# Rotary embedding of queries and keys: the sine half added in DRAM by transfers that exchange the halves

## The chip, the cores and the metric

The kernel runs on one core of a Trainium2 chip. The metric is the device time of one execution in microseconds. Three runs of the kernel before took 2127.07, 2130.25 and 2131.83 us; the median is 2130.25 us.

The engines are named as in the profile: PE multiplies matrices (PEld is its loading of weights), DVE is the vector engine, ACT the scalar engine, POOL is GpSimd, SP is SyncE. Here SP issues nearly all transfers, and POOL issues those that add to what is at their destination.

## The reference

One layer of an encoder on two sequences that share the weights: a long one of 1024 tokens (`x_sample`) and a short one of 512 (`x_prompt`), model width 2048, all in float32. The input is normalised and multiplied by one wide `w_in`, whose columns are split into a convolution group (value, GLU gate, output gate), Q (8 heads of 128), K and V (2 heads each), and an attention gate. The convolution group goes through a depthwise convolution of 31 taps, a layer norm and a 1024 x 1024 product. Q and K are rotated by position; attention looks at bands of 128 tokens on either side, with a sink. Both groups are gated, joined, multiplied by `w_out`, added to the input and normalised. The part that is touched:

```python
def apply_rope(t, pos):
    half = HEAD_DIM // 2
    inv_freq = 1.0 / (ROPE_THETA ** (jnp.arange(half, dtype=jnp.float32) / half))
    ang = pos.astype(jnp.float32)[:, None] * inv_freq[None, :]
    cos = jnp.cos(ang)[None, :, None, :]
    sin = jnp.sin(ang)[None, :, None, :]
    tf = t.astype(jnp.float32)
    t1, t2 = tf[..., :half], tf[..., half:]
    out = jnp.concatenate([t1 * cos - t2 * sin, t2 * cos + t1 * sin], axis=-1)
    return out.astype(t.dtype)
```

## The kernel before

**Layout.** Activations are kept transposed: the 128 channels of a head lie on the 128 partitions, tokens along the row, 512 at a time (`W`). The two halves of a head are therefore rows 0 to 63 and 64 to 127. The table `cos` holds the cosines twice; `sin` holds the sines in its upper half and their negatives in its lower half.

**Products.** Every float32 operand is split into a high part (ACT, line 438) and a low part (DVE, line 439), and three products of the parts are summed on PE. The long sequence is multiplied in blocks of 2 x 2 x 2 with seven products instead of eight (class `Unit`, line 191). One unit takes a pair of column blocks, such as Q of a head and its attention gate, over half of the 2048 input channels. Its seven products leave four sums, one for each half of the tokens (t) and each of the two column blocks (c). In the first pass the sums go to DRAM (`part_...`). In the second pass `finish` (line 240) adds the stored part to the new one with an adding transfer on POOL (`add_into`, line 429) and enters `done` in a list (`later`), which is worked off four products later: for Q and K that is `rotate` (line 943), for gates `silu_of`, for V `value_of`.

**Order.** The second passes of the long sequence stand in the order gates 0 to 3, K and V of two groups, the eight Q units, gates 4 to 7. Then come the products of the short sequence (class `Job`, line 578), the first of them its K, V and Q, each with 48 matrix products, rotated by `rotated` (line 940) straight out of PE's bank. Beside these products run lanes of background work that a clock of estimated costs hands out: the taps of the convolution on DVE (line 906), attention of the long sequence, and preparation. `turn_over` and `behind` tie such work to places in the instruction streams; a scheduler then orders each engine's instructions.

**Buffers.** Tiles named g and u are [128, 512] (four each), taken in turn by `E()`. Tiles of the tag a (four, line 399) hold up to [128, 1024]. Near the end of the second pass, `last_before` (line 1713) loads the normalised input of the short sequence from DRAM (`xr_d`) for splitting: the first eight channel blocks into four a tiles (line 1703), the next four into p tiles (line 1700).

**Rotation before.** `rope` (line 928) multiplies each half of the rows by the sines of the other into b, multiplies all rows by the cosines into o, and adds b to o: four DVE instructions. The result is stored by SP. Q and K are read again later, when attention reaches them.

Of the kernel before, what the change touches and what calls it, by code (L numbers as in the profile page):

```python
# [7 lines left out]
F32 = mybir.dt.float32  # L8
F32R = mybir.dt.float32r
AF = mybir.ActivationFunctionType  # L10
ALU = mybir.AluOpType
PSUM = bass.MemoryType.PSUM

P = 128
# [19 lines left out]
W = 512  # L34
# [619 lines left out]
class Sequence:  # L654
# [270 lines left out]
            nc.vector.tensor_tensor(self.cos, self.cos, self.R, ALU.mult)  # L925
            nc.vector.tensor_tensor(self.sin, self.sin, self.R, ALU.mult)

    def rope(self, acc, c, o=None):
        e, nc = self.e, self.e.nc
        i = slice(c * W, c * W + W)  # L930
        if o is None:
            o = e.G()
        b = e.E()
        nc.vector.tensor_tensor(b[0:64], acc[64:128], self.sin[64:128, i], ALU.mult)
        nc.vector.tensor_tensor(b[64:128], acc[0:64], self.sin[0:64, i], ALU.mult)
        nc.vector.tensor_tensor(o, acc, self.cos[:, i], ALU.mult)
        nc.vector.tensor_tensor(o, o, b, ALU.add)
        return o

    def rotated(self, dst, accs):  # L940
        self.e.store(dst, self.rope(accs[0], 0))

    def rotate(self, dst):
        def done(t, z):
            self.e.store(dst[:, t * W : t * W + W], self.rope(z, t, z))
            yield

        return done
# [902 lines left out]
```

## Time and profile before

The profiled execution took 2123.9 us, of which the span from the first to the last instruction is 2122.1 us, at a granted TensorE clock of 0.998. It is 6.35 us below the median of the three runs.

| engine | busy us | share of the span | instructions |
|---|---|---|---|
| PE | 2080.0 | 98% | 9330 |
| PEld | 1709.6 | 81% | 9330 |
| DVE | 1710.3 | 81% | 2611 |
| ACT | 1064.6 | 50% | 1736 |
| POOL | 105.1 | 5% | 124 |

| stretch (us) | PE busy | DVE busy | DMA share | what runs |
|---|---|---|---|---|
| 640 to 840 | 198.66 | 193.81 | 0.71 | second pass of K, V and Q, long sequence |
| 840 to 870 | 26.83 | 23.79 | 0.94 | last gates; splitting of the short sequence's input |
| 870 to 1050 | 175.54 | 169.64 | 0.52 | K, V and Q of the short sequence, attention of the long one |

How to read it: a share over the whole span mixes stages with different limits. DMA share is the mean busy share of the 16 DMA engines; it can read a little over 1. A wait is idle time of an engine just before an instruction, with what ended it.

### The profile page before, as it was taken

What the parts mean: (1) busy time and instruction counts of PE and PEld (TensorE: products, weight loads), DVE (VectorE), ACT (ScalarE), POOL (GpSimd) and SP (SyncE); (2) the same over time, 40 slices, a digit from 0 to 9 for tenths busy, and PEclk for the clock granted to TensorE, in tenths of its full rate; (3) what the DMA queues carried; (4) which work ended last, traced back from release to release, by engine and by line L of the source; (5) the groups of instructions that cost most, each with busy time, mean ns of one, the idle gap of its engine ahead of it and who ended that gap; (6) DMA issues with size and microseconds to landing.
All of it is one profiled execution on the core that took longest, in us unless ns stands there. A gap on an engine that the chain in (4) does not pass through costs nothing. (4 is left out here: it accounts for less than half of the span.)

```text
span 2122.1 us, 26838 instructions
## 1 busy us (share of the span) xinstructions
PE 2080.0 (98%) x9330; PEld 1709.6 (81%) x9330; DVE 1710.3 (81%) x2611; ACT 1064.6 (50%) x1736; POOL 105.1 (5%) x124
## 2 busy tenths in 40 slices
PE   8999999999999999899999999999999989999998
PEld 7878888888888888688888888878888867888886
DVE  8758799988899999899987776677899667987543
ACT  7475445333554444544556766345544564563232
POOL 0001110000011111000000000000000001110000
PEclk9999999999999999999999999999999999999999
DMA  8888878754677767754464547987765369799952
GB/s 286 310 286 243 231 179 277 265 190 155 227 215 178 185 161 194 240 183 144 151 219 157 192 157 235 323 291 255 249 238 199 105 208 269 192 306 314 309 172 80
DMA packets 236408, 465.17 MB, mean 219 GB/s; under 512 B 22128, under 2 KB 79856, under 8 KB 236272
## 3 DMA queue, kind: packets, MB, share of 16 engines
q1 hardware_dynamic: 218992, 431.99, 60.6%
q0 software_dynamic: 17280, 31.46, 9.0%
q8 instruction: 73, 1.20, 0.2%
q14 instruction: 63, 0.52, 0.1%
HBM read 319.19 MB, written 144.18 MB: 218 GB/s over the span
## 5 line engine op out<-in xcount | busy, mean ns | idle before, releaser
L191 PE MATMUL a<-t,hl 128*128 128x512 f32 x2640 | 634.3, 391 | 15.5 <-ACT u L217 6.0
L191 PEld LDWEIGHTS a<-t,hl 128*128 128x128 f32 x2640 | 494.7, 188 | 123.4 <-ACT u L217 9.2
L438 ACT ACTIVATE hl<-raw 128x1024 fp32r<-128x1024 f32 (+1 forms) x330 | 296.2, 898 | 367.8 <-DVE raw L138 66.7
L439 DVE TENSOR_TENSOR hl<-raw,hl 128x1024 fp32r<-128x1024 f32 (+1 forms) x330 | 337.6, 1023 | 171.0 <-ACT hl L438 167.0
L906 DVE SCALAR_TENSOR_TENSOR f<-f,c_w_dw,f 128x1024 f32<-128x1024 f32 (+1 forms) x464 | 456.0, 1011 | 1.8 <-ACT f L901 1.6
L578 PE MATMUL a<-t,hl 128*128 128x512 f32 x1344 | 329.0, 394 | 2.6 <-DVE f L848 2.2
L191 PE MATMUL c<-t,hl 128*128 128x512 f32 x1320 | 320.1, 390 | 1.6 <-ACT g L217 0.9
L578 PEld LDWEIGHTS a<-t,hl 128*128 128x128 f32 x1344 | 248.8, 188 | 53.8 <-DVE f L848 2.6
L191 PEld LDWEIGHTS c<-t,hl 128*128 128x128 f32 x1320 | 247.4, 188 | 54.0 <-ACT g L217 1.8
L578 PE MATMUL c<-t,hl 128*128 128x512 f32 x672 | 167.4, 395 | 0.0
L578 PE MATMUL b<-t,hl 128*128 128x512 f32 x672 | 162.2, 392 | 0.8 <-DVE hl L439 0.8
L191 PE MATMUL b<-t,hl 128*128 128x512 f32 x660 | 161.1, 390 | 0.0
L578 PEld LDWEIGHTS b<-t,hl 128*128 128x128 f32 x672 | 125.1, 188 | 26.1 <-DVE hl L439 1.2
L578 PEld LDWEIGHTS c<-t,hl 128*128 128x128 f32 x672 | 124.2, 188 | 24.5
L191 PEld LDWEIGHTS b<-t,hl 128*128 128x128 f32 x660 | 123.4, 188 | 25.1
L217 ACT ACTIVATE u<-a 128x512 f32<-128x512 f32 x114 | 67.3, 592 | 77.7 <-PE a L191 64.5
L217 ACT ACTIVATE g<-a 128x512 f32<-128x512 f32 x106 | 62.9, 593 | 80.8 <-PE a L191 68.9
L1534 PE MATMUL a<-hl,t 128*128 128x512 f32 x192 | 74.3, 390 | 0.0
L438 ACT ACTIVATE a<-pt 128x512 fp32r<-128x512 f32 x64 | 38.0, 594 | 62.5 <-PE pt L1058 62.3
L1038 ACT ACTIVATE p<-p,tiny 128x384 f32<-128x384 f32 (+1 forms) x96 | 54.5, 569 | 28.3 <-DVE tiny L1035 19.5
L346 ACT ACTIVATE hl<-raw 128x1024 fp32r<-128x1024 f32 x44 | 46.4, 1053 | 41.1 <-PE a L578 12.7
L439 DVE TENSOR_TENSOR a<-pt,a 128x512 fp32r<-128x512 f32 x64 | 43.9, 686 | 25.3 <-ACT a L438 24.9
(318 smaller groups left out, 2528.2 us busy)
## 6 DMA issues: line engine op xcount, KB each, us to landing
raw<-w_in SPq DMA_DIRECT2D x171, 512.0 KB, 5.0
raw<-w_out SPq DMA_DIRECT2D x64, 256.0 KB, 4.2
raw<-w_out SPq DMA_DIRECT2D x31, 512.0 KB, 4.7
raw<-w_pw SPq DMA_DIRECT2D x24, 512.0 KB, 4.8
p<-xT_s SPq DMA_DIRECT2D x40, 256.0 KB, 4.8
f<-x_s SPq DMA_DIRECT2D x16, 512.0 KB, 7.2
f<-y_d SPq DMA_DIRECT2D x16, 512.0 KB, 5.8
y_s<-f SPq DMA_DIRECT2D x16, 512.0 KB, 4.5
```

What stands on the lines that cost most here:

```text
L191: nc.tensor.matmul(acc, hl[:, l, o, j, :], toks[j][:, r], start=name in FRESH and j == 0 and q == 0, stop=name in LAST and j == HALF - 1 a ...
L217: nc.scalar.activation(t, bank, AF.Copy)
L346: e.nc.scalar.activation(t[:, 0], raw, AF.Copy)
L438: nc.scalar.activation(hi, x, AF.Copy)
L439: nc.vector.tensor_tensor(lo, x, hi.bitcast(F32), ALU.subtract)
L578: nc.tensor.matmul(job.acc[0], hl[:, l, kk // HALF, kk % HALF, :], r, start=i == 0 and p == 0, stop=i == nk - 1 and p == 2,)
L906: nc.vector.scalar_tensor_tensor(t, h[:, j : j + T], w(j), t, ALU.mult, ALU.add)
L1038: nc.scalar.activation(p[:, 0:n], p[:, 0:n], AF.Exp, bias=nm[:, h : h + 1], accum_out=l[:, h : h + 1])
L1534: nc.tensor.matmul(acc, self.mix[self.KS[i]][:, m, b * P : (b + 1) * P], part[l].rearrange("p a b -> p (a b)"), start=i == 0 and p == 0, s ...
```

## The change

The sum of the cosine and sine products moves from DVE into DRAM. `rope` now multiplies all 128 rows by the cosines and all 128 rows by the sines, each row by its own, and adds nothing. `put_rotated` stores the cosine product as before (SP) and then adds to it, with two adding transfers on POOL, the lower half of the sine product to the upper rows and the upper half to the lower rows. For the long sequence the sine product lies in a tile of tag a in place of one from `E()`; for the short sequence it is still one from `E()`.

```diff
-    def rope(self, acc, c, o=None):
-        e, nc = self.e, self.e.nc
+    def rope(self, acc, c, o, b):
+
+        nc = self.e.nc
         i = slice(c * W, c * W + W)
-        if o is None:
-            o = e.G()
-        b = e.E()
-        nc.vector.tensor_tensor(b[0:64], acc[64:128], self.sin[64:128, i], ALU.mult)
-        nc.vector.tensor_tensor(b[64:128], acc[0:64], self.sin[0:64, i], ALU.mult)
+        nc.vector.tensor_tensor(b, acc, self.sin[:, i], ALU.mult)
         nc.vector.tensor_tensor(o, acc, self.cos[:, i], ALU.mult)
-        nc.vector.tensor_tensor(o, o, b, ALU.add)
-        return o
 
     def rotated(self, dst, accs):
-        self.e.store(dst, self.rope(accs[0], 0))
+        e = self.e
+        o, b = e.G(), e.E()
+        self.rope(accs[0], 0, o, b)
+        self.put_rotated(dst, o, b)
+
+    def put_rotated(self, dst, o, b):
+        e, half = self.e, P // 2
+        e.store(dst, o)
+        e.add_into(dst[0:half], b[half:])
+        e.add_into(dst[half:], b[0:half])
 
     def rotate(self, dst):
         def done(t, z):
-            self.e.store(dst[:, t * W : t * W + W], self.rope(z, t, z))
+            b = self.e.A([W], F32)
+            self.rope(z, t, z, b)
+            self.put_rotated(dst[:, t * W : t * W + W], z, b)
             yield
 
         return done
```

POOL's queue in the last Q unit and the first gate unit after it, before the change. The destination is on the left of the arrow; `part_q7_10` is the stored sum of Q head 7, second half of the tokens (1), column block Q (0). Waits on DMAHW are for SP's transfers, on DMASW for POOL's own.

```order
L429 DMA u_887_6976<-part_q7_11_407 128x512 [waits DMAHW1_49,DMASW5_49,DVE_49]
L429 DMA g_883_6936<-part_q7_01_405 128x512 [waits DMASW6_49,DVE_49]
L429 DMA u_893_7025<-part_q7_10_406 128x512 [waits DMAHW1_49,DMASW7_49,Activation_49]
L429 DMA g_897_7047<-part_gate4_00_338 128x512 [waits DMAHW2_49,DMASW0_49,DVE_49]
L429 DMA g_904_7124<-part_gate4_11_341 128x512 [waits DMAHW7_49,DMASW1_49,DVE_49]
L429 DMA u_900_7084<-part_gate4_01_339 128x512 [waits DMAHW4_49,DMASW2_49,DVE_49]
```

The same place in the changed kernel; `a_888` and `a_901` are the sine products of the two halves of the tokens, `q_d0_1` is Q of the second group in DRAM.

```order
L429 DMA u_887_6976<-part_q7_11_407 128x512 [waits DMASW1_49,DVE_49]
L429 DMA u_883_6936<-part_q7_01_405 128x512 [waits DMAHW7_49,DMASW2_49,DVE_49]
L429 DMA g_893_7025<-part_q7_10_406 128x512 [waits DMAHW3_49,DMASW3_49,Activation_49]
L429 DMA q_d0_1_109<-a_888_6980 64x512 [waits DMAHW7_49,DMASW4_49]
L429 DMA q_d0_1_109<-a_888_6980 64x512 [waits DMASW5_49]
L429 DMA u_897_7047<-part_gate4_00_338 128x512 [waits DMASW6_49,DVE_49]
L429 DMA q_d0_1_109<-a_901_7088 64x512 [waits DMAHW5_49,DMASW7_49,DVE_49]
L429 DMA q_d0_1_109<-a_901_7088 64x512 [waits DMASW0_49]
L429 DMA g_904_7124<-part_gate4_11_341 128x512 [waits DMASW1_49,DVE_49]
L429 DMA g_900_7084<-part_gate4_01_339 128x512 [waits DMASW2_49,DVE_49]
```

Two pairs of adding transfers now stand among the additions of partial sums; the first of each pair waits for SP's store of the cosine product.

SP's queue where it loads the short sequence's input into the a tiles, before the change. This is ahead of the K, V and Q units; `xr_d1_0` to `xr_d1_3` are the first four pairs of channel blocks.

```order
L786 DMA a_674_5181<-xT_s 128x512 [waits DMAHW7_49,DVE_49]
L786 DMA a_674_5181<-xT_s 128x512 [waits DMAHW0_49]
L1703 DMA a_908_7166<-xr_d1_0_186 128x1024 [waits DMAHW1_49,DVE_49]
L896 DMA f_758_5876<-h_d0_4_84 128x1024 [waits DMAHW2_49,DVE_49]
L1703 DMA a_909_7168<-xr_d1_1_187 128x1024 [waits DMAHW3_49,DVE_49]
L432 DMA gate_d0_0_88<-u_691_5264 128x512 [waits DMAHW4_49,Activation_49]
L1703 DMA a_910_7170<-xr_d1_2_188 128x1024 [waits DMAHW6_49,DMAHW5_49,DVE_49]
L123 DMA raw_707_5397<-w_in 128x1024 [waits DVE_49]
L1703 DMA a_911_7172<-xr_d1_3_189 128x1024 [waits DMAHW0_49,DMAHW7_49,DVE_49,Activation_49]
```

The same loads in the changed kernel, where their lines are 1709 and 1706. They stand some 75 transfers later, at the end of the last Q unit.

```order
L332 DMA raw_907_7153<-w_in 128x1024 [waits DVE_49]
L1709 DMA a_908_7166<-xr_d1_0_186 128x1024 [waits DMASW5_49,DMAHW3_49,DMASW4_49,DMASW3_49]
L432 DMA ag_d0_7_103<-u_883_6936 128x512 [waits DMAHW4_49,Activation_49]
L432 DMA q_d0_1_109<-g_893_7025 128x512 [waits DMAHW5_49,DVE_49]
L1709 DMA a_909_7168<-xr_d1_1_187 128x1024 [waits DMAHW6_49,DMASW7_49,DMASW0_49]
L1709 DMA a_910_7170<-xr_d1_2_188 128x1024 [waits DMAHW7_49,DMASW5_49,DMASW4_49]
L896 DMA f_960_7408<-h_d0_5_85 128x1024 [waits DMAHW0_49]
L1706 DMA p_912_7174<-xr_d1_4_190 128x512 [waits DMAHW1_49]
L1709 DMA a_911_7172<-xr_d1_3_189 128x1024 [waits DMAHW2_49,DMASW7_49,DMASW0_49]
L432 DMA gate_d0_4_92<-u_897_7047 128x512 [waits DMAHW3_49,Activation_49]
L1706 DMA p_913_7176<-xr_d1_4_190 128x512 [waits DMAHW4_49]
```

The four loads have moved behind the rotations, and the fourth (`a_911`) waits for the two transfers out of `a_901`, the last rotation's sine product. Behind it SP has a gate store, three p loads and a weight load.

## Rows read from the trace of the kernel before

**Rows 1.** The page's busy time: us (share of the span) x instructions.

```profile
PE 2080.0 (98%) x9330; PEld 1709.6 (81%) x9330; DVE 1710.3 (81%) x2611; ACT 1064.6 (50%) x1736; POOL 105.1 (5%) x124
```

**Rows 2.** Waits of PE, 600 to 870 us: total, times, longest.

```profile
PE a L191 <- ACT u L217: 2.4, 2, 1.6
PE a L191 <- DVE hl L439: 1.3, 1, 1.3
PE b L578 <- DVE hl L439: 0.8, 1, 0.8
```

**Rows 3.** Waits of PE, 870 to 1050 us.

```profile
PE s L1024 <- DVE tiny L1027: 2.2, 1, 2.2
PE a L578 <- DVE f L848: 2.2, 1, 2.2
```

**Rows 4.** Stages: engines' busy us (instructions), clock, DMA share, GB/s.

```profile
640.00:840.00 200.00, 198.66 (x883) 163.89 (x882) 193.81 (x263) 84.35 (x127) 35.81 (x41) 1.00 0.71 175
835.00:840.00 5.00, 5.00 (x24) 4.14 (x23) 4.97 (x8) 1.23 (x2) 0.83 (x1) 1.00 1.02 337
840.00:870.00 30.00, 26.83 (x115) 21.02 (x115) 23.79 (x33) 20.27 (x33) 5.32 (x7) 1.00 0.94 270
```

**Rows 5.** Rotation's lines on DVE: count, ns min/median/max, first and last start.

```profile
L934 DVE TENSOR_TENSOR g<-u,f x10: 686/686/689, 665.2 to 831.2; 64x512 f32<-64x512 f32 x10
...
L936 DVE TENSOR_TENSOR u<-u,f x11: 682/685/693, 646.8 to 833.8; 128x512 f32<-128x512 f32 x11
...
L937 DVE TENSOR_TENSOR g<-g,u x14: 677/684/693, 660.9 to 1024.5; 128x512 f32<-128x512 f32 x14
```

**Rows 6.** POOL in order of time, 706 to 740 us.

```profile
715.64 0.88 POOL L429 DMA_DIRECT2D g<-part_q  x1 [6.06 <-DVE g L237]
723.82 0.88 POOL L429 DMA_DIRECT2D g<-part_q  x1 [7.31 <-DVE g L237]
727.17 0.86 POOL L429 DMA_DIRECT2D u<-part_q  x1 [2.47 <-DVE u L237]
727.77 1.15 POOL L429 DMA_DIRECT2D g<-part_q  x1
734.38 0.88 POOL L429 DMA_DIRECT2D u<-part_q  x1 [5.46 <-DVE u L237]
```

**Rows 7.** All engines in order of time, 706 to 726 us.

```profile
717.64 0.69 DVE L934 TENSOR_TENSOR g<-u,f 64x512 f32<-64x512 f32 x1
...
723.45 0.69 DVE L934 TENSOR_TENSOR u<-g,f 64x512 f32<-64x512 f32 x1
```

**Rows 8.** Queues and issues, 640 to 840 us: KB each, us to landing.

```profile
q1 hardware_dynamic: 9919, 24.05, 37.6%
q0 software_dynamic: 5904, 10.75, 33.1%
...
g<-part_q POOLq DMA_DIRECT2D x16, 256.0 KB, 5.4
...
q_d<-g SPq DMA_DIRECT2D x8, 256.0 KB, 2.8
```

**Rows 9.** Transfers that touch xr_d, whole span.

```profile
L1703 SPq DMA_DIRECT2D a<-xr_d x6: 319/324/382, 610.4 to 852.3; - x6
...
DMA to landing us min/median/max: 3.1/5.7/7.2
```

**Rows 10.** All engines in order of time, 836 to 866 us.

```profile
836.33 0.32 SPq L432 DMA_DIRECT2D q_d<-u  x1
...
844.98 3.17 ACT L441 ACTIVATE t<-a,c_norm_g 128x512 fp32r<-128x512 f32 x5
...
847.27 0.69 DVE L882 TENSOR_TENSOR u<-u,f 128x512 f32<-128x512 f32 x1 [1.96 <-DMA u<-part_gate]
...
851.25 0.63 ACT L888 ACTIVATE g<-g 128x512 f32<-128x512 f32 x1 [3.10 <-DVE g L882]
...
853.63 3.01 PE L191 MATMUL a<-t,hl 128*128 128x512 f32 x12 [1.63 <-ACT u L217]
```

## The prediction

> **What bounds the kernel now.** I read the busy shares first. TensorE (PE) is busy 2080.0 of the 2122.1 us [rows 1], so all its idle time together is 42.1 us, and no relief of another engine can give back more. Then I asked where PE waits in the part of the program that rotates anything, 600 to 1050 us. From 600 to 870 it waits 1.3 us for a weight split on VectorE (DVE), 2.4 us in two pieces for ScalarE (ACT) to empty a bank, and 0.8 us for another split [rows 2]. From 870 to 1050 it waits twice, 2.2 us each, both times for DVE [rows 3]. These five lines sum to 8.9 us; that is the most that can be gained here by any means. Third, the stages. From 640 to 840, where K and Q of the long sequence are rotated, DVE is busy 193.81 of 200 us, PE 198.66, and the DMA engines 0.71 of their time [rows 4]. So DVE is nearly full, but PE hardly waits for it: full is not late. At the end of that stretch the picture turns: from 840 to 870 the DMA share is 0.94 and PE is busy only 26.83 of 30 us, and the 5 us before it (835 to 840) already have a DMA share of 1.02 [rows 4].
>
> **What the change removes and adds on DVE.** There are 30 rotations: 20 for the long sequence (K and Q, two halves each), 10 for the short one. Before, each is two 64-row products at 0.686 us, one 128-row product at 0.685 us and one sum at 0.684 us [rows 5]: 2.74 us. After, it is two 128-row products. A 64-row product costs what a 128-row one does, so a rotation becomes 1.37 us, and 30 of them save 41 us of DVE: 27 us between 640 and 840, 14 us after 870. What hangs on it is the 6.5 us that PE waits for DVE in 600 to 1050 (1.3 + 0.8 + 2.2 + 2.2). The 0.8 and the two 2.2 come after 860, behind work that no rotation precedes closely, and conv taps move up into the room that is freed. I count only the 1.3 us wait, which stands among the rotations, and where the new order of PE no longer runs two units into each other: **-1.3 us**, bounds 0 and -6.5.
>
> **What it adds on GpSimd's queue (POOL).** Each rotation now has two more transfers there, 60 in all, and the first waits until the cosine product has landed in DRAM. Behind it in the same queue stand the additions of partial sums, which DVE needs some 8 us later (the one issued at 715.64 [rows 6] is rotated at 723.45 [rows 7]). One unit of 18.7 us decides: its four additions are issued at 715.64, 723.82, 727.17 and 727.77 (the last lasts 1.15), the next unit's first at 734.38 [rows 6]. The rotation at 717.64 [rows 7] ends with two products at 719.0; the store lands in 2.8 [rows 8], at 721.8; two issues of 0.87 end at 723.5, before 723.82. The rotation at 723.45 [rows 7] ends at 724.8, has landed at 727.6, waits until 728.9 for the addition ahead of it, and its issues end at 730.7, before 734.38. So the new pair fits in both gaps: **0 us**. In units 0, 1, 4 and 6 the pair stands one place earlier and delays an addition by about 3 us. With its landing of 5.4 [rows 8] that is 8.4 us against 7.8, so DVE may stall for 0.6 us; it has been given 2.7 us per unit, which hides that.
>
> **What it adds to the DMA engines.** Additions into DRAM of 64 rows are not in this trace. The nearest row is the 128-row addition into SBUF: the software queue takes 33.1% of 16 engines over 200 us [rows 8], 1059 us for 41 of them, 25.8 us each. At half the rows a new one is 12.9 us, and 40 of them put 516 us on 3200: the share goes from 0.71 to 0.87. From above, I double it, because the sum is read from and written to DRAM: 1.03, that is 3% too much for the stage, +6 us. From below I take a packet of the hardware queue, 37.6% of 3200 us over 9919 packets, 121 ns against 179 [rows 8]: the share is 0.82. I take 0.87 and **0 us**: 0.87 still leaves the engines idle between the units, and at 0.94, from 840 to 870, the longest of PE's waits is for ACT [rows 2, 4].
>
> The plain store into DRAM (q_d) lands in 2.8 us, the addition into SBUF in 5.4 [rows 8]; I take the latter for the new transfers. The Trainium skill (DMA: Bandwidth & Descriptors, Anatomy of one DMA) says that completion is mostly the write receipt, heaviest where the target is HBM; the rows here show the opposite order, the store into DRAM being the sooner. By the rule alone a new addition would land later than 5.4 us, by at most the 2 us that the page gives for it (an estimate), and the fourth load of the next part would come at about 852. The same page (Rules for kernel authors) says that two transfers of disjoint partition halves gain nothing over one of 128 rows, since both use the same 16 engines; no run here shows that yet, and by it the load would be the 25.8 us per pair used above.
>
> **What it moves: the handover.** This is the step I worry about. The sine products of the long sequence live in buffers of the tag a, of which there are four. Before, the same four were free early, and the first eight pieces of the short sequence's input (four loads of 512 KB, xr_d) went into them from 610 us on [rows 9]. After, each load waits for the additions out of a rotation's sine product, the fourth for the very last rotation, and it stands in SyncE's (SP's) queue ahead of a gate store, three more loads and a weight load. Its time: the last store is issued at 836.33 [rows 10]; two products fewer make that 835.0; landed at 837.8; the second addition is issued at 838.7 and lands at 844.1; the load takes 5.7 [rows 9]: 849.8 us. Before, ACT took its two pieces as the last of the five that began at 844.98, 0.63 us each, so from 846.9. So it is 2.9 us late. But ACT then sat idle for 3.10 us, until 851.25, behind DVE [rows 10], so the delay just fits. Past that point it goes one for one into ACT's next emptying of a bank, and so into PE's wait for it, 1.63 us before 853.63 [rows 10]. And 2.1 MB more arrive in just the stretch whose DMA share is already 1.02. At its 337 GB/s [rows 4] they are 6.2 us. DVE's wait of 1.96 us for a partial sum at 847.27 [rows 10] stands in the same crowd, and sets that chain too. From below: if DVE's lag shrinks and the partial sum is added earlier, the two ACT waits (2.4 us) could go; from above, all 6.2 us come late. The cover is used up by what I can count, so I take a quarter of the upper end: **+1.5 us**.
>
> For the short sequence, the bank is given back two DVE operations sooner and the sine product is held some 10 us longer, in one of four buffers, while a job lasts 10.9 us: 0 us either way.
>
> **The sum**, on the profiled execution's own 2123.9 us (span 2122.1): -1.3 + 0 + 0 + 1.5 = +0.2, so 2124.1. The median of the runs shown, 2130.25, is 6.35 above that execution; on the median the forecast is **2130.5 us**. Something under 0.2% (4.3 us) can't be told from no change here.
>
> **The rivals.** (A) *The handover decides.* The additions or the load land in the crowd, ACT is held past 851.25, and PE waits at 853. For: DMA share 1.02 and a queue position behind the last rotation. Against: DVE runs earlier, which moves everything here forward. It decides as soon as the fourth load lands after some 850 us, and costs the 6.2 us of added traffic less the 1.3 gained, 4.9, or 10 if the partial sum that follows is late by as much again and only the 2.4 us of ACT waits hide part of it (2 x 6.2 - 2.4): 2135 to 2140. (B) *The DMA engines saturate in 640 to 840*, if an addition into DRAM costs double or more: partial sums and weights land late. At double the share is 1.03, at 2.3 times 1.08, so 3 to 8% of 200 us is lost: 2136 to 2146. For: 0.71 is already high, and that price is not in the trace. Against: plain stores into DRAM are the quickest transfers there. (C) *DVE was the hidden limit.* Its relief removes most of the 8.9 us: 2121.3 to 2125.5. For: DVE at 97% in the stage. Against: PE waits 1.3 us in those 200 us.
>
> **How the numbers follow.** The forecast, within 4.3 us of 2130.25, gets 0.57; A 0.17, B 0.10, C 0.16. Hence faster 0.16, same 0.57, slower 0.27. The range reaches over C and to the top of A and the lower half of B: 2121 to 2142; the forecast's own range is 2126 to 2134.5.
>
> **What would show it.** DVE's busy time falls by 41 us to about 1669, with 60 rotation products near 0.69 us. PE's waits in 640 to 840 stay under 2 us, and the 1.3 us wait for a split is gone. POOL shows the new pairs in the gaps named, and no partial sum waits for them. The DMA share of the stage is near 0.87; near 1.0 speaks for B. The fourth load lands near 850, and PE's gap at 853 tells A from the forecast: 1 to 3 us there is the forecast, 5 or more is A. I am wrong in kind if PE loses time in the prompt's rotations or after 1050 us, where I see nothing that changes.

## The result, and the profile after

The changed kernel takes 2138.42 us (median; 2135.69 to 2145.35), the kernel before, run beside it, 2130.25 us. The ratio is 1.0037, with a 95% interval of 1.0026 to 1.0049: slower by 8 us, where I had forecast no change. The time lies in the range, on the side to which I had given 0.27. The profiled execution took 2139.14 us (span 2137.4, granted clock 0.995).

The page's busy times, after:

```profile
PE 2085.0 (98%) x9330; PEld 1711.9 (80%) x9330; DVE 1668.7 (78%) x2551; ACT 1063.8 (50%) x1736; POOL 156.6 (7%) x184
```

DVE has lost 41.6 us against [rows 1]. The stages, in the columns of [rows 4]:

```profile
640.00:840.00 200.00, 193.04 (x851) 157.46 (x850) 161.21 (x216) 80.20 (x124) 68.01 (x78) 1.00 0.83 188
840.00:870.00 30.00, 24.65 (x101) 19.61 (x100) 22.70 (x32) 16.80 (x28) 5.25 (x6) 0.89 1.01 313
870.00:1050.00 180.00, 175.02 (x813) 141.75 (x812) 152.75 (x222) 88.50 (x157) 17.71 (x21) 1.00 0.70 195
```

PE is busy 5.6 us less in the rotations' stage and 2.2 us less in the 30 us behind it, where its granted clock is 0.89 as well; from 870 to 1050 there is 0.5 us between the two. The two profiled executions differ by 15.2 us and the medians by 8.2, mostly because the one before lies 6.35 us below its median. To place the loss, I compare when the matrix product of the same number starts in both: after the change PE loses 7.3 us from 604 to 831 us (times of before) and 4.5 more up to 927, next to nothing up to 1355, and 4.0 behind that, where nothing was changed. The second run with the additions behind the sums, below, loses 4.7 us there, though it is faster than the kernel before; so those 4 us are not put down to the change. PE's waits from 600 to 870 us, for [rows 2]:

```profile
PE a L191 <- ACT u L217: 9.8, 4, 5.3
PE a L191 <- DVE hl L439: 1.3, 1, 1.3
PE a L191 <- ACT g L217: 1.2, 2, 0.7
```

They were 4.5 us and are 12.3. The longest of them and two others, PE alone in order of time:

```profile
708.02 2.57 PE L191 MATMUL a<-t,hl 128*128 128x512 f32 x10 [1.33 <-DVE hl L439]
715.73 3.02 PE L191 MATMUL a<-t,hl 128*128 128x512 f32 x12 [2.43 <-ACT u L217]
...
864.28 4.68 PE L191 MATMUL a<-t,hl 128*128 128x512 f32 x12 [5.34 <-ACT u L217]
```

ACT empties the banks (line 217) late; why, DVE's rows say. The first product of the rotation, in groups over 640 to 840 us (last columns: idle time ahead of it and what ended it):

```profile
L932 DVE TENSOR_TENSOR a<-g,f 128x512 f32<-128x512 f32 x10 | 6.9, 691 | 13.2 <-DMA g<-part_kv 7.1 <-issue 4.2 <-DMA g<-part_q 1.8
...
L932 DVE TENSOR_TENSOR a<-u,f 128x512 f32<-128x512 f32 x10 | 6.9, 690 | 17.1 <-issue 13.7 <-DMA u<-part_q 2.8 <-DMA u<-part_kv 0.6
```

DVE, which has less to do, stands still for 30.3 us ahead of 20 rotations. ("issue" names no releaser, but each of the five products with such a wait starts 0.08 us after a partial sum lands.) POOL's groups show who is queued. Before, 640 to 840 us:

```profile
L429 POOL DMA_DIRECT2D g<-part_q x16 | 14.7, 922 | 63.7 <-DVE g L237 63.6 <-issue 0.2
L429 POOL DMA_DIRECT2D u<-part_q x16 | 14.6, 911 | 62.3 <-DVE u L237 54.3 <-DMA q_d<-g 8.0
```

and after:

```profile
L429 POOL DMA_DIRECT2D q_d<-a x30 | 26.5, 1001 | 79.6 <-DVE u L237 21.9 <-DVE a L932 17.2 <-DVE raw L138 9.0
L429 POOL DMA_DIRECT2D g<-part_q x16 | 17.3, 1213 | 7.6 <-DVE g L237 3.1 <-issue 2.3 <-DVE hl L439 1.4
L429 POOL DMA_DIRECT2D u<-part_q x16 | 17.1, 1172 | 10.1 <-DVE u L237 4.1 <-issue 2.6 <-ACT hl L438 1.6
```

Here idle time is good news. Before, POOL idled 126 us ahead of 32 partial sums: it was there first, and a sum went out the moment it was ready. After, it idles 17.7 us ahead of them: the sums are ready first, and stand behind a rotation's additions, ahead of which POOL now spends its idle time. The rows put much of that time down to DVE; but 17 of the 20 pairs start 0.53 to 0.63 us after a store of a rotation lands, so it is the store that they wait for. One such case, all engines in order of time:

```profile
686.67 0.60 ACT L217 ACTIVATE u<-a 128x512 f32<-128x512 f32 x1 [0.59 <-PE a L191]
687.84 0.32 SPq L432 DMA_DIRECT2D q_d<-u  x1
...
693.10 1.68 POOL L429 DMA_DIRECT2D q_d<-a  x2 [3.42 <-DMA q_d<-u]
694.29 1.42 POOL L429 DMA_DIRECT2D u<-part_q  x1
...
704.34 0.69 DVE L932 TENSOR_TENSOR a<-u,f 128x512 f32<-128x512 f32 x1 [8.04 <-issue]
...
708.02 2.57 PE L191 MATMUL a<-t,hl 128*128 128x512 f32 x10 [1.33 <-DVE hl L439]
708.80 0.63 ACT L438 ACTIVATE hl<-raw 128x512 fp32r<-128x512 f32 x1 [7.37 <-DVE raw L138]
709.41 1.69 POOL L429 DMA_DIRECT2D q_d<-a  x2 [12.79 <-DVE u L237]
710.58 2.40 POOL L429 DMA_DIRECT2D u<-part_q  x2
```

ACT has emptied the bank by 687.3. The cosine product, stored at 687.84, lands 5 us later; until then the pair of additions holds POOL, and the partial sum goes out at 694.29, 7 us after it was ready. It lands behind the pair's data, and DVE waits for it until 704.34. Behind that product on DVE wait the weight combinations (line 138) and splits (439), so ACT stands 7.37 us and PE 1.33. The late rotation is stored late, at 706.86, and its pair stands ahead of the next two sums, of which the first was ready at 709.3 and goes out at 710.58. The queues and landings of 640 to 840 us, for [rows 8]:

```profile
q0 software_dynamic: 8777, 15.43, 49.8%
q1 hardware_dynamic: 9097, 21.99, 33.0%
...
raw<-w_in SPq DMA_DIRECT2D x20, 512.0 KB, 7.3
u<-part_q POOLq DMA_DIRECT2D x16, 256.0 KB, 7.0
g<-part_q POOLq DMA_DIRECT2D x16, 256.0 KB, 6.9
q_d<-a POOLq DMA_DIRECT2D x30, 128.0 KB, 5.7
```

And the handover, all engines in order of time, for [rows 10]:

```profile
841.29 0.32 SPq L432 DMA_DIRECT2D q_d<-g  x1
...
843.08 0.69 DVE L237 TENSOR_TENSOR g<-u,g 128x512 f32<-128x512 f32 x1
...
848.92 1.68 POOL L429 DMA_DIRECT2D q_d<-a  x2 [9.96 <-DVE raw L138]
850.06 2.37 POOL L429 DMA_DIRECT2D g<-part_gate  x2
...
854.06 0.32 SPq L1709 DMA_DIRECT2D a<-xr_d  x1
...
856.76 0.69 DVE L882 TENSOR_TENSOR g<-g,f 128x512 f32<-128x512 f32 x1 [3.21 <-DMA g<-part_gate]
...
860.67 1.33 ACT L441 ACTIVATE t<-a,c_norm_g 128x512 fp32r<-128x512 f32 x2 [5.67 <-DMA a<-xr_d]
```

Two things are late at once ahead of PE's 5.34 us at 864: the gates' partial sums behind the last pair, and the load behind the last additions. The first of those sums is ready at 843.8 and goes out at 850.06, 6.3 us later, because the last rotation's store, issued at 841.29, lands only at 848.4.

### The profile page after: what moved, and what is told of

It is laid out like the page before. It is cut to its first block, busy times and chain, and to the rows that moved or that the text cites. A ratio compares the mean times of both kernels' runs of the same rounds, so it can differ in the third digit from the quotient of the medians.

```text
span 2137.4 us, 26915 instructions
## 1 busy us (share of the span) xinstructions
PE 2085.0 (98%) x9330; PEld 1711.9 (80%) x9330; DVE 1668.7 (78%) x2551; ACT 1063.8 (50%) x1736; POOL 156.6 (7%) x184
## 5 line engine op out<-in xcount | busy, mean ns | idle before, releaser
L191 PE MATMUL a<-t,hl 128*128 128x512 f32 x2640 | 636.6, 392 | 22.5 <-ACT u L217 12.3
L346 ACT ACTIVATE hl<-raw 128x1024 fp32r<-128x1024 f32 x44 | 46.4, 1054 | 46.7 <-PE b L578 15.2
L429 POOL DMA_DIRECT2D u<-part_out x16 | 14.0, 890 | 756.5 <-DVE t L439 697.4
```

The source lines that it names most:

```text
L191: nc.tensor.matmul(acc, hl[:, l, o, j, :], toks[j][:, r], start=name in FRESH and j == 0 and q == 0, stop=name in LAST and j == HALF - 1 a ...
L346: e.nc.scalar.activation(t[:, 0], raw, AF.Copy)
L429: self.nc.gpsimd.dma_start(dst, src, accum_op=ALU.add)
```

## The experiments

Three theories. **Q** (queue): a rotation's additions wait on POOL for a store, and hold up the partial sums behind them. **L** (load): the added transfers make every transfer of the stage slower; landings are up by as much as 2 us. **H** (handover): the late loads of the short sequence's input. Each run's ratio is to the kernel before, run beside it.

**Early loads.** In `rotate`:

```diff
-            b = self.e.A([W], F32)
+            b = self.e.E()
```

> The sine products of the long sequence lie in g and u tiles instead of a tiles; all else as changed. The four loads of the short sequence's input then go back to their early place in SP's queue (transfer 386 instead of 460). Theory H (the handover: loads that wait for the last rotation's additions): PE's 5.3 us wait near 864 us and the slow products behind it go, so 4 to 5 us of the 8.2 us come back: 2133.5 to 2134.5. Theory Q (on POOL's queue a rotation's additions wait for a store and hold up the partial sums behind them) and theory L (the added transfers make every transfer of the stage slower) have nothing to do with where the sine product lies: 2138, and PE busy for 193 us of 640 to 840 as after the change.

Measured: 2139.77 us, ratio 1.0038 (1.0025 to 1.0051). Nothing came back, and PE's wait is still there:

```profile
847.32 1.68 POOL L429 DMA_DIRECT2D q_d<-g  x2 [10.17 <-DVE u L237]
848.56 1.37 POOL L429 DMA_DIRECT2D g<-part_gate  x1
...
857.63 0.69 DVE L882 TENSOR_TENSOR u<-u,f 128x512 f32<-128x512 f32 x1 [6.66 <-DMA u<-part_gate]
...
864.00 4.80 PE L191 MATMUL a<-t,hl 128*128 128x512 f32 x12 [7.52 <-ACT u L217]
```

The gates' partial sums behind the last pair are enough to make it: the first is ready at 841.9 and goes out at 848.56, behind a pair whose store lands at 846.8. So the gap does not need late loads. As a test of the whole loss the run isn't clean: PE is busy 195.41 us in 640 to 840, 2.4 more than after the change, and sine products in g and u tiles have a price of their own, as the run with both at once shows. What clears H as the main cause are the next two runs, in which the loads stand about as late in SP's queue as after the change.

**No wait for the store.** The additions go where nothing has to land first (`old` is the unit's partial sum in DRAM; the line that keeps it is left out here):

```diff
-            self.put_rotated(dst[:, t * W : t * W + W], z, b)
+            self.e.store(dst[:, t * W : t * W + W], z)
+            self.e.add_into(old[0 : P // 2], b[P // 2 :])
+            self.e.add_into(old[P // 2 :], b[0 : P // 2])
```

> The 20 rotations of the long sequence add their sine products, in the same two transfers of 64 x 512 on POOL, into the unit's own used-up partial sum in DRAM instead of onto the stored cosine product (so the long sequence's Q and K lack their sine half). The transfers and their load stay, the wait for the store goes. Theory Q: DVE's waits at the rotation's first product (28 us in 640 to 875 after the change) shrink to under 8, PE is busy some 198 of 200 us in 640 to 840, and some 6 of the 8.2 us come back: about 2132. Theory L: same load, same time, 2138, PE busy 193 us in 640 to 840. Theory H: the last additions are issued only some 3 us sooner, so 2136 to 2138, and PE still waits over 3 us near 860.

Measured: 2129.24 us, ratio 0.9995 (0.9983 to 1.0007): all of the loss is gone, with the same additions.

```profile
640.00:840.00 200.00, 199.38 (x887) 164.66 (x887) 168.78 (x227) 84.88 (x131) 70.95 (x82) 1.00 0.87 205
...
L933 DVE TENSOR_TENSOR a<-u,f 128x512 f32<-128x512 f32 x10 | 6.9, 687 | 1.1 <-issue 0.6 <-DMA u<-part_kv 0.5
...
L933 DVE TENSOR_TENSOR a<-g,f 128x512 f32<-128x512 f32 x10 | 6.8, 683 | 0.7 <-DMA g<-part_q 0.7
```

PE is busier than before the change, at a higher DMA share (0.87) than after it (0.83). L falls, and Q holds, in place (DVE idles 1.8 us ahead of the rotations' first products, against 30.3 after the change) as in size. DVE is idle in other places instead, 24.3 us of it ahead of weight splits that wait for ACT, and PE loses nothing by that: the 30.3 us were no measure of the loss, only a sign of where it arose. Two more things go with the wait: the additions have another destination, and the fourth of the loads is issued at 839 us, not 854. The next run keeps the destination.

**Additions behind the sums.** The same additions at the same destinations, in another order on POOL (`add_halves` makes the two additions of a pair; `pairs` keeps them until the unit's last sum is issued):

```diff
+            if n == (1, 0):
+                last = e.nc.cur_bb.bb.instructions[-1]
+                while e.pairs:
+                    with e.tc.issue_after(last):
+                        e.add_halves(*e.pairs.popleft())
...
-            self.put_rotated(dst[:, t * W : t * W + W], z, b)
+            self.e.store(d, z)
+            self.e.pairs.append((d, b))
```

> The additions of the long sequence's rotations are put, by an edge in POOL's order, behind the last of the four partial sums of the unit in which the rotation falls: two pairs in one place, once per unit, where the store has long landed. Theory Q: no partial sum is held up, PE is busy 197 us or more in 640 to 840, and 6 us come back there; but the last pair is then issued behind the last partial sum of the first gate unit, near 853 us, so the handover gets later, and by theory H up to 8 us are lost there: 2132 to 2140, with PE's wait near 860 at 5 to 13 us. Theory L: PE busy 193 us in 640 to 840, 2138 or more.

Measured: 2126.49 us, ratio 0.9982 (0.997 to 0.9995), faster than both kernels. The loss at the handover that H asked for did not come; the last pair went out at 840 us, not near 853. A second time, beside two variants below:

> The kernel with the additions behind the unit's last partial sum once more, beside the two variants on one chip: 2126.5, ratio to before 0.998. Theory H wants the two variants 3 to 5 us below it, theory Q alone within 1 us of it.

Measured: 2127.89 us, ratio 0.9984 (0.9975 to 0.9994). The stages of the first run, and its POOL groups over 640 to 840 us:

```profile
640.00:840.00 200.00, 200.00 (x891) 165.60 (x890) 167.47 (x226) 84.47 (x131) 69.72 (x81) 1.00 0.89 205
840.00:870.00 30.00, 25.09 (x101) 20.02 (x101) 21.12 (x30) 18.33 (x31) 5.54 (x7) 0.89 1.03 304
```

```profile
L435 POOL DMA_DIRECT2D q_d<-a x30 | 28.8, 1464 | 0.1
L435 POOL DMA_DIRECT2D g<-part_q x16 | 14.0, 875 | 47.6 <-DVE g L237 44.2 <-ACT g L217 3.4
L435 POOL DMA_DIRECT2D u<-part_q x16 | 14.0, 872 | 50.8 <-DVE u L237 46.1 <-ACT u L217 4.7
```

No addition of a rotation waits any more (0.1 us), POOL is ahead of the sums again, and PE never stops in 200 us. A partial sum lands in 4.5 us here, sooner than the 5.4 before the change [rows 8]; why sooner than there, no run shows. No run has a higher DMA share than its 0.89. One wait of PE is left up to 870 us, at 854:

```profile
PE a L191 <- ACT u L217: 4.9, 1, 4.9
```

**Is that one the late loads'?** Three runs on H. The kernel before, with its b in an a tile:

```diff
-        b = e.E()
+        b = e.A([W], F32) if o_given else e.E()
```

> The kernel before, with the long sequence's sine products in a tiles: no adding transfer, DVE as busy as before, but the four loads of the short sequence's input stand at transfer 461 of SP's queue instead of 386. Theory H: late loads alone cost 1.5 to 5 us: 2131.5 to 2135, and PE waits 3 us or more near 855. Theory Q: nothing, 2130, PE waits 1.6 us there as before.

Measured: 2130.01 us, ratio 1.0003 (0.9994 to 1.0013). PE alone:

```profile
855.92 4.60 PE L191 MATMUL a<-t,hl 128*128 128x512 f32 x12 [3.09 <-ACT u L217]
```

The late loads do lengthen that wait, 3.09 us against 1.63 [rows 10], and slow products follow; the median doesn't show it, though its interval leaves room for 2.8 us.

Behind the sums, with b in the p tiles, so that the loads are early: `b = self.e.PT("p", NP, [W])`.

> Additions behind the unit's last partial sum, with the long sequence's sine products in p tiles (four) instead of a tiles; the a loads are early (transfer 386), g and u tiles are as before. Theory H: the 4.9 us wait near 854 us and the slow products behind it were the late loads': PE waits under 2 us there, and the time is 2121 to 2124. Theory Q alone: late loads cost nothing in the end (the kernel before with late loads took no longer), 2126 to 2127. Rival: the four p tiles are wanted by the weight combinations too (line 145) and by four loads of 256 KB near 845 us, which now wait for the last additions: PE waits move to 640 to 840 or past 860, 2128 or more.

Measured: 2126.74 us, ratio 0.9988 (0.9975 to 1.0).

```profile
858.23 3.04 PE L191 MATMUL a<-t,hl 128*128 128x512 f32 x12 [2.18 <-ACT u L217]
```

The wait shrinks to 2.18 us, and the time stays: Q alone.

Behind the sums, with the last two Q units rotated as before (`if old:` store `rope_old(z, t, z)`).

> As with the additions behind the unit's last partial sum, but the last two Q units (four rotations) are rotated as before the change, so that the a tiles are free some 40 us sooner (transfers 448 to 455 of SP's queue). Theory H: 2121 to 2124, PE's wait near 854 us under 2 us. Theory Q alone: 2126 to 2127, as with all rotations behind the sums; DVE gets 5.5 us more work, which may show as waits of PE before 860 us.

Measured: 2130.95 us, ratio 0.9992 (0.9979 to 1.0005). The wait, at 857, is 1.16 us, but another comes up in the stretch of the last Q units, for a tile that is still being stored:

```profile
818.25 0.60 ACT L217 ACTIVATE g<-c 128x512 f32<-128x512 f32 x1 [6.95 <-DMA ag_d<-g]
818.89 1.58 PE L191 MATMUL c<-t,hl 128*128 128x512 f32 x5 [3.72 <-ACT g L217]
```

So this run tells nothing of H; its ratio can't be told from behind's.

**Both at once, in g and u tiles.** Behind the sums, with `b = self.e.E()`.

> Both pairs of additions behind the unit's last partial sum, and the sine products in g and u tiles, so that the loads of the short sequence's input are early again. Theory Q+H (held-up partial sums cost the 6 us before 840 us, late loads the rest after it): PE is busy 199 us or more in 640 to 840, the 4.9 us wait that is left near 854 us with the additions behind the sums goes, and the time is 2120 to 2123. Theory Q alone (late loads cost nothing; what is left near 854 us is the gates' partial sums): 2126, the wait of some 5 us stays. Rival theory E (the sine products, held some 15 us, use up the eight g and u buffers, so that ACT waits to empty banks): 2128 to 2135, PE waits for ACT in 640 to 840.

Measured: 2135.08 us, ratio 1.002 (1.0003 to 1.0036): rival E. PE is busy 195.12 of 200 us, with waits for ACT of 2.0 and 2.6 us; ahead of the second, ACT had waited 5.83 us to write a g tile:

```profile
701.92 0.60 ACT L217 ACTIVATE g<-a 128x512 f32<-128x512 f32 x1 [5.83 <-issue]
```

The row does not name what it waits for. The tag of b is all in which this run differs from the one with p tiles, and 0.14 us before ACT starts, at 701.78, an addition out of a g tile lands that had been issued at 693.42; so the tile is the likely reason.

**The short sequence alone.** The long one is rotated as before (`rope_old` is the `rope` of before):

```diff
-            b = self.e.A([W], F32)
-            self.rope(z, t, z, b)
-            self.put_rotated(dst[:, t * W : t * W + W], z, b)
+            self.e.store(dst[:, t * W : t * W + W], self.rope_old(z, t, z))
```

> The long sequence is rotated as before the change, only the ten rotations of the short sequence add in DRAM. All three theories place the cost in the long sequence's part: 2130 (2128.5 to 2131.5). If the short sequence's rotations cost or gain something of their own, 2132 or more, or 2128 or less.

Measured: 2128.27 us, ratio 0.999 (0.9979 to 1.0002). No cost there; there are no partial sums on POOL in that stage.

**The price of an addition.** One of 128 rows in place of each pair: `self.e.add_into(old, b)`.

> As the run in which the additions go to the used-up partial sum, but each pair of 64 x 512 is one addition of 128 x 512 (so no halves are exchanged, and the long sequence's Q and K lack their sine half). It prices a DRAM addition by its rows. In 640 to 840 us POOL's queue takes 49.0% of the 16 engines with pairs, 33.1% with none. If a pair costs twice its halves for nothing (a fixed cost per transfer), one addition of 128 rows leaves the share near 41 to 43%; if only the bytes count, it stays at 48 to 50%, and DMA's share in the stage at 0.86 to 0.87. Time by theory Q 2127 to 2131, since nothing waits for a store.

Measured: 2125.93 us in a single run, without an interval; POOL's queue in 640 to 840 us:

```profile
q0 software_dynamic: 8786, 16.00, 50.4%
```

The bytes count. At 25.8 us for a partial sum, the price of before, and 42 of them, 529 us are left for 20 additions, 26.5 us each; in the run of pairs (49.0%) 484 us for 40, 24.2 a pair. The Trainium skill (DMA: Bandwidth & Descriptors, Rules for kernel authors) says that two transfers of disjoint partition halves gain nothing over one of 128 rows; these two runs agree.

## Why the prediction was right or wrong, point by point

- **DVE, -1.3 us.** The work was right: 41.6 us, products of 0.69. That its relief is worth little was nearly right, and can only be seen where nothing is held up: with the additions behind the sums PE does without the 1.3 us wait, and the kernel is 0.18% (some 4 us) faster than before, inside my bounds of 0 and -6.5. I had counted nothing for the two waits of [rows 3]; in the two profiles with the additions behind the sums PE's waits from 870 to 1050 us are down from 4.4 to 2.0 and 2.4 us, while the one near 854 is longer. How these make up the 4 us can't be told from single profiles.
- **POOL's queue, 0 us: this step failed.** I had seen it ("in units 0, 1, 4 and 6 the pair stands one place earlier and delays an addition by about 3 us") and priced it at 0.6 us, hidden. Measured is a sum held for 7 us and 30.3 us of DVE's waits, and without the wait for the store 9 us come back (ratio 0.9995 against 1.0037). I had taken both landings, 2.8 and 5.4, from a queue without the change; with it they are 3.4 to 3.5 (5 in the case shown) and 7.0. And I had worked out one unit from the times of before, as if each unit began afresh; but a late sum makes a late rotation, a late store and a late pair, ahead of the next sums, as in the case shown. How much of the loss is this feedback no run tells apart.
- **DMA share, 0.87, 0 us.** Right: 0.83 after the change, 0.87 to 0.89 where nothing is held up, and PE busy 199.4 to 200.0 of 200 us at that share. An addition of 64 rows takes 12.1 to 15.4 us of the 16 engines in three runs (my 12.9). Rival B, a stage limited by its transfers, is out. The sums' later landings are mostly order: a partial sum lands in 7.0 us behind pairs that wait, in 5.6 to 5.9 behind pairs that don't (the run without the wait), and in 4.5 ahead of them. The plain stores of Q do land later where nothing is held up, in 4.4 to 5.8 us against 2.8 before, but no partial sum stands behind them there.
- **Handover, +1.5 us.** In size right for the loads alone, PE's wait there growing by 1.5 us when only they are late; but that is luck, since I had taken a quarter of an upper end. The sign in the profile, a gap of 5 us or more there (at 864, for the 853 of before), was the one that I had named for rival A, and the time fell into A's 2135 to 2140. A part of the loss does stand where A puts it, 4.5 of the 11.8 us that the profile after loses up to 927. But A's traffic and late loads are not the main cause: with the loads early the gap was longer (7.52 us), with them late and nothing else changed the time did not move, and with the additions behind the sums PE, product by product, loses only 0.6 and 1.8 us from 831 to 927 in the two profiles, at DMA shares of 1.03 and 1.02. The gap at 864 is mostly the queue's too, its last case. So the measured time lies in my range for a reason that none of the range's rivals gives.
- **The short sequence, 0 us.** Right, within 0.2%.

## What to carry to other kernels

A transfer that waits for another transfer holds up the issues behind it in its engine's queue (on POOL here a partial sum for 7 us); count what stands behind it, and put it behind the work that is ready sooner. Whether it fits into a gap must be worked out with the landing times of the changed kernel, and over several turns of the loop, where its delay feeds back into its own start. Idle time of a queue ahead of an issue says that the issue was not late; when it vanishes from a group, that group is being held up.

## What had not been expected of the hardware

After PE's long waits the products behind them are slow as well: 12 of them took 4.68 us after the 5.34 us wait, 4.60 after 3.09 and 4.80 after 7.52, but 3.01 after 1.63 us (before the change) and 3.02 after 2.43. The granted clock of the 10 us from 860, after the change, averages 0.66, between its two levels, 2.4 and 1.2 GHz; from 862 to 867 it reads 0.50, the lower one:

```profile
860.00:870.00 10.00, 5.72 (x18) 4.59 (x19) 9.10 (x14) 7.64 (x13) 0.88 (x1) 0.66 1.05 378
```

So such a wait cost some 1.6 to 1.8 us more than the row that names it says.
